# Two two-layer models on one core: mixer biases on GpSimd, a prepared final norm, reordered attention steps

## The chip, the core and the metric

The kernel runs on one core of a Trainium2 chip. The metric is device time in microseconds (us). TensorE (PE) does matmuls and transposes into PSUM (eight banks); VectorE (DVE) and ScalarE (ACT) do the rest; GpSimd (POOL) does small powers, some products and some transfers; the SP queue issues most transfers.

## The reference

Two models of two layers each, 256 positions, width 1024, fp32. `norm` is an RMS norm, `ffn` a gated feed-forward of width 2816.

```
for l in 0, 1:                                   # first model
    x = x + 0.5 * ffn(norm(x))
    p = norm(x) @ w_in + b_in                    # 5792 columns: three branches and 3 x 1024 gates
    y_a = lru_branch(p) @ lru_w_out
    y_b = latent_attention(p) @ mla_w_o          # 8 heads
    y_c = conv_branch(p) @ conv_w_out + conv_b_out
    x = x + (sig(g0) * y_a + sig(g1) * y_b + sig(g2) * y_c) @ w_out
    x = x + 0.5 * ffn(norm(x))
x = norm(x)                                      # second model
x = x + dilated_attention(norm(x)) @ a_w_out     # three dilations (1, 4, 16), each with its q, k, v; 16 heads,
                                                 # merged by their log-denominators
x = x + ffn(norm(x))
h = norm(x) @ b_w_in                             # q, k, v of 16 heads, and 16 columns of forget gates
c = cumsum(log_sigmoid(h[gates] + b_f))
x = x + attention(q, k, v, bias c_i - c_j) @ b_w_out
x = x + ffn(norm(x))
out = norm(x)
```

## The kernel before

All of x lies in SBUF as two tiles (t) of 128 positions. A matrix product is made in three passes: a weight slab of 128x1024 is loaded by SP (`raw`, five buffers), ACT rounds it to `H` (L378), DVE subtracts the rest `L` (L380), and PE multiplies H and L with the input's rounded part and H with its rest. `tm` has the input stationary and up to 512 weight columns moving, into two PSUM banks (one for each t) out of a ring; `fm` has the weights stationary. The stages follow one another: feed-forward, mixer, feed-forward, twice; the dilated attention; feed-forward; the forgetting attention ("fox"); feed-forward; the final norm.

In a **mixer** the order of the steps is the string `ORDER`. `gB`, `gA`, `gC` make the gates of the three branches (halves 0 and 1 of the columns), `yB`, `yA`, `yC` their output products (`combine`), summed in M. A gate is kept as tanh, so a branch adds (tanh + 1) times its product; M is halved later. `gate` loads its bias row of 1024 at half 0 into `bg`, which has one buffer; `combine_c` loads the convolution's bias into the same buffer and DVE adds it to the product (L917) ahead of the multiplication (L919) and the sum (L921). `pump` works off taps of the convolution on DVE (L861), `cn`, `cv`, `co` normalise it; `cv` ends in a power on POOL (`pow_rs`, L461). Two banks at a time come from a ring of three. Behind the last step M is transposed for `w_out`.

In **both attention stages** the steps of a group of heads are posted as jobs and run one by one between weight slabs (`tick`): `T` transposes q and k, `SC` makes scores, maximum and exponentials `P`, `U` transposes P and copies it to `PT`, `V` multiplies with v and normalises, `R` transposes the output and splits it. In dilations 4 and 16 (`banded`) four heads go together, in dilation 1 (`full`) and in fox (`pairs`) two. PE takes its instructions in the order written (`InOrder`); the other engines are ordered by the tile scheduler. In these stages `T`, `U` share a ring of two banks (3 and 6), `SC` has banks 4 and 5, `V` bank 7; `R` uses a strip of banks 4 and 5. In fox, `forget` makes the 16 gate columns with `tm` and their logarithms; `rows` makes the running sum and spreads it over the partitions through DRAM.

The **final norm** squares x (ACT, with a sum), takes a power on POOL for each t (`norm_scale`), and scales x times the gain.

Of the kernel before, what the change touches and what calls it, by code (L numbers as in the profile page):

```python
# [11 lines left out]
F32 = mybir.dt.float32  # L12
# [3 lines left out]
AF = mybir.ActivationFunctionType  # L16
# [3 lines left out]
S = 256  # L20
# [14 lines left out]
ORDER = ("rb glu:0 conv4:0 glu:1 latent conv4:1 lt gelu:0 pump:43 gelu:1 k:0 q:0 rk q:1 rq pump:6 lg:0 narrow "  # L35
         "gB:0 lg:1 k:1 pump:5 lg:2 lg:3 h:0 lru pump:14 gB:1 gA:0 h:1 h:2 h:3 gA:1 yB:0 yA:0 gC:0 yB:1 "
         "pump:52 cn cv yA:1 co gC:1 yC:0 yC:1")

# [205 lines left out]
class K:  # L244
# [217 lines left out]

    def norm_scale(self, t):
        nc, x = self.nc, self.x
        ss = self.sp.tile([128, 2], F32, name="ss1")
        ms = self.sp.tile([128, 1], F32, name="ms1")
        r = self.sp.tile([128, 1], F32, name="r1")
        for h in range(2):
            scr = self.sp.tile([128, 512], F32, name="scr", bufs=1)
            nc.scalar.activation(scr, x[:, t, 512 * h:512 * h + 512], AF.Square, accum_out=ss[:, h:h + 1])  # L470
        nc.vector.tensor_add(ms, ss[:, 0:1], ss[:, 1:2])
        nc.vector.tensor_scalar(ms, ms, 1.0 / D, EPS, op0=OP.mult, op1=OP.add)
        self.pow_rs(r, ms)
        return r

    def norm(self, gain):
# [218 lines left out]
    def mixer(self, l):  # L695
# [201 lines left out]
        def gate(b, i, n):  # L897
            j = (1, 0, 2)[i]
            if n == 0:
                bg[0] = p.tile([128, D], F32, name="bg", bufs=1)  # L900
                self.row(bg[0], A["b_in"], l * 5792 + 2720 + 1024 * j, D)
            g = gt[b]
            ns = slice(512 * n, 512 * n + 512)
            ps, = self.tm("w_in", l, [10 + 2 * i + n], XH, XL)
            for t in range(2):
                nc.vector.scalar_tensor_tensor(g[:, t, ns], ps[t], r[:, t:t + 1], bg[0][:, ns], op0=OP.mult, op1=OP.add)
            nc.scalar.activation(g[:, :, ns], g[:, :, ns], AF.Tanh, scale=0.5)

        def combine(name, b, YH, YL, n, bias=None):
            g = gt[b]  # L910
            ns = slice(512 * n, 512 * n + 512)
            ps, = self.tm(name, l, [n], YH, YL)
            for t in range(2):
                gs, src = g[:, t, ns], ps[t]
                if bias is not None:
                    y = ta.rearrange("p j s -> p (j s)")
                    nc.vector.tensor_add(y, ps[t], bias[:, ns])  # L917
                    src = y
                nc.vector.scalar_tensor_tensor(gs, gs, 1.0, src, op0=OP.add, op1=OP.mult)  # L919
                if b:  # L920
                    nc.vector.tensor_add(M[:, t, ns], M[:, t, ns], gs)  # L921

        def combine_c(n):
            if n == 0:
                bg[1] = p.tile([128, D], F32, name="bg", bufs=1)
                self.row(bg[1], A["conv_b_out"], l * D, D)
            combine("conv_w_out", 1, ycH, ycL, n, bias=bg[1])

# [7 lines left out]
            "yB": lambda n: combine("mla_w_o", 0, oH, oL, n), "yA": lambda n: combine("lru_w_out", 1, yaH, yaL, n),  # L936
            "yC": combine_c,
        }
# [25 lines left out]
    def final_norm(self, out):  # L964
        nc, x, g, xg = self.nc, self.x, self.gain, self.xg
        r = [self.norm_scale(t) for t in range(2)]
        for h in range(2):
            hs = slice(512 * h, 512 * h + 512)
            for t in range(2):
                nc.vector.tensor_mul(xg[:, t, hs], x[:, t, hs], g[:, hs])  # L970
        for t in range(2):
            for h in range(2):
                xs = xg[:, t, 512 * h:512 * h + 512]
                if h:
                    nc.vector.tensor_scalar(xs, xs, r[t], None, op0=OP.mult)
                else:
                    nc.scalar.activation(xs, xs, AF.Copy, scale=r[t])
                nc.sync.dma_start(out[0, 128 * t:128 * t + 128, 512 * h:512 * h + 512], xs)
        self.fin[0].close()
# [19 lines left out]
    def dilated(self):  # L999
# [59 lines left out]
        def banded(g, dil, hf, q, k):  # L1059
# [61 lines left out]

            early = [lambda: T(0), lambda: (T(1), SC(0)), lambda: (U(0), SC(1))]
            return early, lambda v: [lambda: (V(0, v), U(1)), lambda: (V(1, v), leave())]

        def full(hf, q, k):
# [27 lines left out]
            def U(i):  # L1153
                PT[i] = p.tile([128, 2, 2, 2, 128], F32, name="PT", bufs=2).rearrange("p a b c d -> p (a b c d)")[:, :768].rearrange("p (h c) -> p h c", h=2)
                for e in range(2):
                    tp = self.pt()[:, :384]
                    for b in range(3):
                        self.pe.transpose(tp[:, 128 * b:128 * b + 128], P[i][:, e, 128 * b:128 * b + 128], self.ident)
                    nc.vector.tensor_copy(PT[i][:, e], tp)  # L1159

# [31 lines left out]
            def R(i):  # L1192
                pb = self.bank[:, 4:6, 384:512]
                for t in range(2):
                    self.pe.transpose(pb[:, t], O[i][:, t], self.ident)
                h, lo = (z[:, 4 * hf + i].rearrange("p (t s) -> p t s", t=2) for z in (OH, OL))
                nc.scalar.copy(h, pb)
                nc.vector.tensor_sub(lo, pb, h.bitcast(F32))  # L1198

            early = [lambda: T(0), lambda: (T(1), SC(0)), lambda: (U(0), SC(1), T(2))]  # L1200
            return early, lambda v: [lambda: (V(0, v), U(1), SC(2), T(3)), lambda: (V(1, v), U(2), SC(3)),
                                     lambda: (V(2, v), R(0), U(3)), lambda: (V(3, v), R(1)), lambda: R(2), lambda: R(3)]

# [57 lines left out]
    def fox(self):  # L1261
# [10 lines left out]
        z = p.tile([128, 2, NH], F32, name="z")  # L1272

        def forget():
            e = p.tile([128, 2, NH], F32, name="e")
            ps, = self.tm("b_w_in_2", 0, [6], self.XH, self.XL)
            for t in range(2):
                nc.vector.scalar_tensor_tensor(z[:, t], ps[t], r[:, t:t + 1], bf, op0=OP.mult, op1=OP.add)
            nc.vector.scalar_tensor_tensor(e, z, -1.0, z, op0=OP.mult, op1=OP.max)
            nc.scalar.activation(e, e, AF.Exp, scale=-1.0)  # L1280
            l1p = self.log1p_exp(p, e.rearrange("p t h -> p (t h)"), 2 * NH, "lf")
            nc.vector.scalar_tensor_tensor(z, z, 0.0, l1p.rearrange("p (t h) -> p t h", t=2), op0=OP.min, op1=OP.subtract)
# [30 lines left out]
        def pairs(hf, q, k):  # L1313
# [12 lines left out]
            def SC(i):  # L1326
                P[i] = p.tile([128, 2, 384], F32, name="P", bufs=2)
                nm = p.tile([128, 2, 2], F32, name="nm", bufs=2)
# [18 lines left out]
            def U(i):  # L1347
                PT[i] = p.tile([128, 2, 384], F32, name="PT", bufs=2)
                for e in range(2):
                    tp = self.pt()[:, :384]  # L1350
                    for n in range(3):
                        self.pe.transpose(tp[:, 128 * n:128 * n + 128], P[i][:, e, 128 * n:128 * n + 128], self.ident)
                    nc.scalar.copy(PT[i][:, e], tp)

# [12 lines left out]
            def R(i):  # L1367
                pb = self.bank[:, 4:6, 384:512]
                for t in range(2):
                    self.pe.transpose(pb[:, t], O[i][:, t].rearrange("p h d -> p (h d)"), self.ident)  # L1370
                h, lo = (z[:, 4 * hf + i].rearrange("p (t s) -> p t s", t=2) for z in (OH, OL))
                nc.scalar.copy(h, pb)
                nc.vector.tensor_sub(lo, pb, h.bitcast(F32))

            early = [lambda: T(0), lambda: (SC(0), T(1)), lambda: (U(0), SC(1), T(2))]
            return early, lambda v: [lambda: (V(0, v), U(1), SC(2), T(3)), lambda: (V(1, v), U(2), SC(3)), lambda: (V(2, v), R(0), U(3)),
                                     lambda: (V(3, v), R(1)), lambda: R(2), lambda: R(3)]

        forget()
        self.post(5, rows)  # L1380
        for hf in range(2):
            late = []

            def each(i, a, q, k, v, hf=hf, late=late):
                if i == 1:
# [3 lines left out]
                    for n, job in enumerate(early):  # L1389
                        self.post((3 if hf else 5) + n, job)  # L1390
                if i == 2:
                    if hf == 0:
                        self.psum("pipe")
                    for job in late[0](v):
                        self.post(2, job)
            self.qkv(p, "b_w_in_2", 3 * hf, r, r8, HD, each=each)
# [66 lines left out]
```

## Time and profile before

| | us |
|---|---|
| median of three runs (2052.47 to 2054.57) | 2053.25 |
| profiled execution, its own time | 2052.71 |
| its span, first to last instruction | 2050.9 |
| PE busy | 2016.4 (98%) |
| DVE busy | 1314.3 (64%) |
| ACT busy | 1074.4 (52%) |
| POOL busy | 50.4 (2%) |

Busy time is that of instructions in work; matmuls are pipelined and their ends are modelled, so a stretch of full PE need not be PE at its highest rate. The mean granted clock of TensorE was 0.996 of full speed. A wait is the idle time of an engine ahead of an instruction, and the releaser is what ended it.

### The profile page before, as it was taken

Reading aid. Unit: us, or ns where it says so; the run is one execution under the profiler, and the core shown is the slowest. Engines: PE = TensorE matmul, PEld = TensorE weight load, DVE = VectorE, ACT = ScalarE, POOL = GpSimd, SP = SyncE. Lnnn points to the kernel's source line nnn. Section 1 sums busy time; section 2 is a strip of 40 time slices with the busy share of each in tenths; the row PEclk is TensorE's granted clock in tenths of the full one; section 3 lists DMA queues with packets and bytes.
Section 4 is the critical chain, followed back from the end, with each engine's and each line's share of the span. In section 5 each row is a group of like instructions: output and inputs, shape, how many; then the busy total and the mean of one; then the engine's idle time right before and its main releaser. Section 6 shows DMA issues by size and latency. Waiting matters only on the chain.

```text
span 2050.9 us, 27543 instructions
## 1 busy us (share of the span) xinstructions
PE 2016.4 (98%) x10496; PEld 1700.3 (83%) x10496; DVE 1314.3 (64%) x1994; ACT 1074.4 (52%) x1570; POOL 50.4 (2%) x70
## 2 busy tenths in 40 slices
PE   8999999999999999999999999999999999999998
PEld 7888988788888888988788887888778888788886
DVE  4565999865545556999755556666775555555554
ACT  5444685554445445675554456454554444555443
POOL 0000000000000000000000000000220000000000
PEclk9999999999999999999999999999999999999999
DMA  7566554556565556554556564555335564435653
GB/s 223 184 206 198 183 168 154 183 174 187 182 191 182 187 183 210 161 177 162 167 183 186 184 195 144 166 188 173 118 109 185 185 185 156 175 114 184 186 184 124
DMA packets 101700, 358.12 MB, mean 175 GB/s; under 512 B 13328, under 2 KB 14384, under 8 KB 101312
## 3 DMA queue, kind: packets, MB, share of 16 engines
q1 hardware_dynamic: 97312, 348.41, 53.9%
q0 software_dynamic: 4112, 7.72, 1.2%
q8 instruction: 82, 1.34, 0.3%
q10 hardware_dynamic: 144, 0.24, 0.1%
q14 instruction: 50, 0.41, 0.1%
HBM read 352.68 MB, written 3.23 MB: 174 GB/s over the span
## 4 chain that ended last, share of the span: by engine, by line
PE 84%; DVE 7%; issue 5%; ACT 3%; DMA 1%; POOL 0%; POOLq 0%; ACTq 0%; DVEq 0%
PE bank L215 80%; PE bank L218 4%; DVE L L380 2%; ACT H L378 1%; DVE acc L861 1%; DMA bg<-in_conv_b_out 0%; DVE xa L803 0%; DMA pi<-in_positions 0%; DMA h<-in_masks 0%; ACT XN L1031 0%; ACT P L1150 0%; DVE fr L457 0%; ACT cs L889 0%; DVE ta L917 0%; ACT XH L456 0%
## 5 line engine op out<-in xcount | busy, mean ns | idle before, releaser
L380 DVE TENSOR_TENSOR L<-raw,H 128x1024 fp32r<-128x1024 f32 (+1 forms) x653 | 794.0, 1217 | 644.3 <-ACT H L378 642.4
L378 ACT CAST H<-raw 128x1024 fp32r<-128x1024 f32 (+1 forms) x653 | 682.5, 1046 | 829.0 <-PE bank L215 796.2
L215 PE MATMUL bank<-H,XH 128*128 128x512 f32 (+3 forms) x1680 | 636.0, 379 | 2.7 <-ACT H L378 2.6
L215 PE MATMUL bank<-L,XH 128*128 128x512 f32 (+3 forms) x1680 | 630.1, 375 | 1.1 <-DVE L L380 1.1
L215 PE MATMUL bank<-H,XL 128*128 128x512 f32 (+3 forms) x1680 | 627.0, 376 | 0.0
L215 PEld LDWEIGHTS bank<-H,XH 128*128 128x128 f32 x1680 | 316.9, 189 | 58.6 <-ACT H L378 2.8
L215 PEld LDWEIGHTS bank<-L,XH 128*128 128x128 f32 x1680 | 317.2, 189 | 55.7 <-DVE L L380 2.7
L215 PEld LDWEIGHTS bank<-H,XL 128*128 128x128 f32 x1680 | 315.7, 189 | 55.8 <-DVE XL L457 1.4
L215 PE MATMUL bank<-H,HH 128*128 128x512 f32 x528 | 206.5, 391 | 0.0
L215 PE MATMUL bank<-H,HL 128*128 128x512 f32 x528 | 205.5, 389 | 0.0
L215 PE MATMUL bank<-L,HH 128*128 128x512 f32 x528 | 205.4, 389 | 0.0
L215 PEld LDWEIGHTS bank<-H,HL 128*128 128x128 f32 x528 | 99.1, 188 | 20.8
L215 PEld LDWEIGHTS bank<-H,HH 128*128 128x128 f32 x528 | 99.5, 188 | 20.1
L215 PEld LDWEIGHTS bank<-L,HH 128*128 128x128 f32 x528 | 99.2, 188 | 20.2
L861 DVE SCALAR_TENSOR_TENSOR acc<-cpad,cvec,acc 128x256 f32<-128x256 f32 x240 | 104.2, 478 | 0.0
L215 PE MATMUL bank<-H,XP 128*128 128x512 f32 x256 | 85.0, 403 | 0.2 <-DVE XP L1198 0.2
L215 PE MATMUL bank<-XH,H 128*128 128x256 f32 x256 | 70.9, 282 | 0.1
L215 PE MATMUL bank<-XH,L 128*128 128x256 f32 x256 | 71.0, 280 | 0.0
L215 PE MATMUL bank<-XL,H 128*128 128x256 f32 x256 | 70.1, 281 | 0.0
L215 PE MATMUL bank<-H,XN 128*128 128x512 f32 x192 | 63.1, 398 | 0.0
L215 PEld LDWEIGHTS bank<-H,XP 128*128 128x128 f32 x256 | 48.7, 191 | 11.2 <-DVE XP L1198 0.8
L215 PEld LDWEIGHTS bank<-v,PT 128*128 128x128 f32 x416 | 51.7, 191 | 3.7 <-DVE PT L1159 0.7
(333 smaller groups left out, 2027.9 us busy)
## 6 DMA issues: line engine op xcount, KB each, us to landing
raw<-in_ffn_w SPq DMA_DIRECT2D x264, 512.0 KB, 3.5
raw<-in_ffn_w_gu SPq DMA_DIRECT2D x88, 512.0 KB, 3.6
raw<-in_w_in SPq DMA_DIRECT2D x80, 512.0 KB, 3.5
raw<-in_a_w_in SPq DMA_DIRECT2D x72, 512.0 KB, 3.7
raw<-in_ffn_w_down SPq DMA_DIRECT2D x44, 512.0 KB, 3.6
raw<-in_b_w_in SPq DMA_DIRECT2D x24, 512.0 KB, 3.5
raw<-in_w_out SPq DMA_DIRECT2D x16, 512.0 KB, 3.5
raw<-in_mla_w_o SPq DMA_DIRECT2D x8, 512.0 KB, 3.5
```

The lines of the kernel that those rows point to most:

```text
L215: self._next(self.tc.nc.tensor.matmul(*args, **kw))
L218: self._next(self.tc.nc.tensor.transpose(*args, **kw))
L378: nc.scalar.copy(H[:, :nw], raw[:, :nw])
L380: nc.vector.tensor_sub(L[:, :nw], raw[:, :nw], H[:, :nw].bitcast(F32))
L861: nc.vector.scalar_tensor_tensor(acc[:, c], cpad[:, c, tap:tap + S], dww[:, tap, c:c + 1], acc[:, c], op0=OP.mult, op1=OP.add)
```

## The change

In the mixers a gate's bias comes as two halves of 512, and `bg` has two buffers. Two new steps stand in `ORDER`: `bM` loads half of the convolution's bias and adds it to M on POOL; `bC` multiplies it on POOL with the gate and adds that to M. DVE's addition of the bias (L917) goes. In the final norm the first halves are squared for both tiles first and their part of the mean is kept in `pre`. In `banded`, `full` and `pairs` the parts of the jobs are in another order, half of the PT copies change engine, and R of odd heads uses the ring of T and U. In fox `forget` has the weights stationary and the arithmetic on its result is a job of its own (`gates`); U comes one job later, with a third buffer for P; the jobs of the second half of the heads are posted earlier.

```diff
-         ... gA:1 yB:0 yA:0 gC:0 yB:1 pump:52 cn cv yA:1 co gC:1 yC:0 yC:1
+         ... gA:1 yB:0 yA:0 gC:0 bM:0 bC:0 yB:1 pump:52 cn cv yA:1 bM:1 co gC:1 yC:0 bC:1 yC:1
...
         def gate(b, i, n):
-            if n == 0:
-                bg[0] = p.tile([128, D], F32, name="bg", bufs=1)
-                self.row(bg[0], A["b_in"], l * 5792 + 2720 + 1024 * j, D)
+            bias = p.tile([128, 512], F32, name="bg", bufs=2)
+            self.row(bias, A["b_in"], l * 5792 + 2720 + 1024 * j + 512 * n, 512)
...
+        def bias(n):
+            ns = slice(512 * n, 512 * n + 512)
+            bg[n] = p.tile([128, 512], F32, name="bg", bufs=2)
+            self.row(bg[n], A["conv_b_out"], l * D + 512 * n, 512)
+            for t in range(2):
+                nc.gpsimd.tensor_add(M[:, t, ns], M[:, t, ns], bg[n])
+        def gate_bias(n):
+            ns = slice(512 * n, 512 * n + 512)
+            tb = ta.rearrange("p j s -> p (j s)")
+            for t in range(2):
+                m = M[:, t, ns]
+                nc.gpsimd.tensor_mul(tb, gt[1][:, t, ns], bg[n])
+                nc.gpsimd.tensor_add(m, m, tb)
...
-                gs, src = g[:, t, ns], ps[t]
-                if bias is not None:
-                    y = ta.rearrange("p j s -> p (j s)")
-                    nc.vector.tensor_add(y, ps[t], bias[:, ns])
-                    src = y
-                nc.vector.scalar_tensor_tensor(gs, gs, 1.0, src, op0=OP.add, op1=OP.mult)
+                gs = g[:, t, ns]
+                nc.vector.scalar_tensor_tensor(gs, gs, 1.0, ps[t], op0=OP.add, op1=OP.mult)
...
     def final_norm(self, out):
-        r = [self.norm_scale(t) for t in range(2)]
         for h in range(2):
+            for t in range(2):
+                nc.scalar.activation(scr, x[:, t, hs], AF.Square, accum_out=ss[:, t, h:h + 1])
+                if h:
+                    nc.vector.scalar_tensor_tensor(ms[:, t:t + 1], ss[:, t, 1:2], 1.0 / D, pre[:, t:t + 1], op0=OP.mult, op1=OP.add)
+                    self.pow_rs(r[t], ms[:, t:t + 1])
+                else:
+                    nc.vector.tensor_scalar(pre[:, t:t + 1], ss[:, t, 0:1], 1.0 / D, EPS, op0=OP.mult, op1=OP.add)
...
         def banded(g, dil, hf, q, k):
-            early = [lambda: T(0), lambda: (T(1), SC(0)), lambda: (U(0), SC(1))]
+            early = [lambda: T(0), lambda: (T(1), SC(0)), lambda: (SC(1), U(0))]
...
         def full(hf, q, k):                      # U; R is changed alike in pairs
-                    nc.vector.tensor_copy(PT[i][:, e], tp)
+                    (nc.vector.tensor_copy if e else nc.scalar.copy)(PT[i][:, e], tp)
-                pb = self.bank[:, 4:6, 384:512]
+                pb = self.pt()[:, :S].rearrange("p (t s) -> p t s", t=2) if i % 2 else self.bank[:, 4:6, 384:512]
-            early = [lambda: T(0), lambda: (T(1), SC(0)), lambda: (U(0), SC(1), T(2))]
-            return early, lambda v: [lambda: (V(0, v), U(1), SC(2), T(3)), lambda: (V(1, v), U(2), SC(3)),
+            early = [lambda: T(0), lambda: (T(1), SC(0)), lambda: (T(2), SC(1), U(0))]
+            return early, lambda v: [lambda: (T(3), SC(2), V(0, v), U(1)), lambda: (SC(3), V(1, v), U(2)),
                                      lambda: (V(2, v), R(0), U(3)), lambda: (V(3, v), R(1)), lambda: R(2), lambda: R(3)]
...
         def forget():
-            ps, = self.tm("b_w_in_2", 0, [6], self.XH, self.XL)
+            ps = self.pt()[:NH, :S]
+            H, L = self.slab("b_w_in_2", 0, 6, 0, 8)
+            for k in range(8):
+                self.pe.matmul(ps, H[:, k, :], self.XH[:, k, :], start=k == 0, stop=False)
+                self.pe.matmul(ps, L[:, k, :], self.XH[:, k, :], start=False, stop=False)
+                self.pe.matmul(ps, H[:, k, :], self.XL[:, k, :], start=False, stop=k == 7)
+            nc.vector.tensor_copy(zt, ps)
+        def gates():
+            for t in range(2):
+                self.pe.transpose(ps[:, t], zt[:, 128 * t:128 * t + 128], self.ident[:NH, :NH])
...
         def pairs(hf, q, k):
-                P[i] = p.tile([128, 2, 384], F32, name="P", bufs=2)
+                P[i] = p.tile([128, 2, 384], F32, name="P", bufs=3)
-                    nc.scalar.copy(PT[i][:, e], tp)
+                    (nc.vector.tensor_copy if e else nc.scalar.copy)(PT[i][:, e], tp)
-            early = [lambda: T(0), lambda: (SC(0), T(1)), lambda: (U(0), SC(1), T(2))]
-            return early, lambda v: [lambda: (V(0, v), U(1), SC(2), T(3)), lambda: (V(1, v), U(2), SC(3)), lambda: (V(2, v), R(0), U(3)),
-                                     lambda: (V(3, v), R(1)), lambda: R(2), lambda: R(3)]
+            early = [lambda: T(0), lambda: (T(1), SC(0)), lambda: (T(2), SC(1))]
+            return early, lambda v: [lambda: (T(3), SC(2), U(0)), lambda: (V(0, v), SC(3), U(1)), lambda: (V(1, v), U(2)),
+                                     lambda: (V(2, v), R(0), U(3)), lambda: (V(3, v), R(1)), lambda: (R(2), R(3))]
         forget()
+        self.post(2, gates)
         self.post(5, rows)
-                        self.post((3 if hf else 5) + n, job)
+                        self.post((2 if hf else 5) + n, job)
-                        self.post(2, job)
+                        self.post(2 - hf, job)
```

## Rows read from the trace of the kernel before

**Rows 1.** Stretches: us; PE, PEld, DVE, ACT, POOL busy (instructions); clock; DMA share; GB/s.

```profile
206.00:412.00 206.00, 203.38 (x1204) 178.41 (x1205) 189.83 (x350) 131.27 (x219) 3.37 (x4) 1.00 0.54 169
430.00:617.00 187.00, 187.00 (x901) 156.95 (x900) 100.71 (x103) 88.87 (x107) 0.69 (x1) 1.00 0.60 186
...
1221.00:1532.00 311.00, 300.83 (x1654) 246.45 (x1653) 211.11 (x421) 166.76 (x276) 30.32 (x38) 0.99 0.48 151
...
1720.00:1857.00 137.00, 131.63 (x762) 109.09 (x760) 78.37 (x160) 78.06 (x161) 2.39 (x4) 0.98 0.43 143
```

**Rows 2.** Waits of PE, whole span: us in total, times, longest.

```profile
PE bank L218 <- DVE PT L1159: 4.8, 2, 2.4
PE bank L218 <- ACT P L1345: 2.9, 3, 1.6
...
PE bank L218 <- DVE gt L921: 2.1, 2, 1.0
PE bank L218 <- ACT v L991: 1.7, 1, 1.7
PE bank L218 <- DVE XP L1198: 1.6, 2, 1.3
...
PE bank L218 <- ACT P L1089: 1.3, 1, 1.3
...
PE bank L215 <- DVE ta L917: 1.1, 2, 0.7
```

**Rows 3.** Two stretches of the first mixer, DVE alone; columns as in rows 1.

```profile
344.00:364.00 20.00, 19.79 (x33) 1.00 0.64 203
364.00:404.00 40.00, 30.30 (x39) 1.00 0.59 183
```

**Rows 4.** Timeline, end of the first mixer: start, us, engine, line, operation [idle before].

```profile
393.43 0.33 SPq L295 DMA_DIRECT2D bg<-in_conv_b_out  x1
...
398.52 0.69 DVE L917 TENSOR_TENSOR ta<-bank,bg 128x512 f32<-128x512 f32 x1 [1.72 <-DMA bg<-in_conv_b_out]
...
399.27 0.50 PE L215 MATMUL bank<-H,ycH 128*128 128x512 f32 x1 [0.73 <-DVE ta L917]
...
399.86 1.22 DVE L380 TENSOR_TENSOR L<-raw,H 128x1024 fp32r<-128x1024 f32 x1
```

**Rows 5.** Timeline of POOL in the dilated stage.

```profile
1441.65 1.18 POOL L1187 TENSOR_TENSOR O<-Y,w 128x256 f32<-128x256 f32 x2 [24.80 <-DVE w L1183]
...
1445.14 2.17 POOL L1187 TENSOR_TENSOR O<-Y,w 128x256 f32<-128x256 f32 x2 [1.49 <-DVE w L1183]
```

**Rows 6.** Timeline of DVE at the same time.

```profile
1445.31 1.52 DVE L380 TENSOR_TENSOR L<-raw,H 128x1024 fp32r<-128x1024 f32 x1
```

**Rows 7.** Timeline of PE in the dilated stage, second half of the heads.

```profile
1501.07 0.44 PE L218 MATMUL bank<-ident,q 128*128 128x128 f32 x2 [2.45 <-DVE PT L1159]
```

**Rows 8.** Stretches of PE alone, dilated stage and start of fox; clock is third.

```profile
1502.00:1505.00 3.00, 3.00 (x8) 0.50 0.26 104
1727.00:1734.00 7.00, 7.00 (x23) 0.52 0.14 35
```

**Rows 9.** Timeline of PE in fox, matmuls of `forget`, first and last of 29.

```profile
1723.64 0.26 PE L215 MATMUL bank<-H,XH 128*128 128x16 f32 x1
...
1726.77 0.26 PE L215 MATMUL bank<-L,XH 128*128 128x16 f32 x1
```

**Rows 10.** A stretch of the first mixer in which PE runs 256-column matmuls.

```profile
207.00:230.00 23.00, 23.00 (x199) 1.00 0.58 178
```

**Rows 11.** Timeline of the final norm.

```profile
2042.95 0.69 DVE L568 SCALAR_TENSOR_TENSOR x<-bank,x 128x512 f32<-128x512 f32 x1
...
2044.37 0.19 ACT L470 ACTIVATION_READ_ACCUMULATOR scr<-x 128x1 f32 x1
...
2045.50 0.15 DVE L472 TENSOR_SCALAR ms<-ms 128x1 f32<-128x1 f32 x1
...
2045.73 0.55 POOL L461 TENSOR_TENSOR r<-ms,half 128x1 f32<-128x1 f32 x1 [0.66 <-DVE ms L472]
```

More of the change, by code (lines that the diff above doesn't have):

```diff
@@ L35 @@
 ORDER = ("rb glu:0 conv4:0 glu:1 latent conv4:1 lt gelu:0 pump:43 gelu:1 k:0 q:0 rk q:1 rq pump:6 lg:0 narrow "
-         "gB:0 lg:1 k:1 pump:5 lg:2 lg:3 h:0 lru pump:14 gB:1 gA:0 h:1 h:2 h:3 gA:1 yB:0 yA:0 gC:0 yB:1 "
-         "pump:52 cn cv yA:1 co gC:1 yC:0 yC:1")
+         "gB:0 lg:1 k:1 pump:5 lg:2 lg:3 h:0 lru pump:14 gB:1 gA:0 h:1 h:2 h:3 gA:1 yB:0 yA:0 gC:0 bM:0 bC:0 yB:1 "
+         "pump:52 cn cv yA:1 bM:1 co gC:1 yC:0 bC:1 yC:1")
 def _span(a, b, w):
@@ L461, in pow_rs @@
         self.nc.gpsimd.tensor_tensor(out, ms, self.half[:, 0:1].to_broadcast([128, n]), op=OP.pow)
[L463 to L474, printed above, removed]
     def norm(self, gain):
@@ L905, in gate, with combine @@
             for t in range(2):
-                nc.vector.scalar_tensor_tensor(g[:, t, ns], ps[t], r[:, t:t + 1], bg[0][:, ns], op0=OP.mult, op1=OP.add)
+                nc.vector.scalar_tensor_tensor(g[:, t, ns], ps[t], r[:, t:t + 1], bias, op0=OP.mult, op1=OP.add)
             nc.scalar.activation(g[:, :, ns], g[:, :, ns], AF.Tanh, scale=0.5)
-        def combine(name, b, YH, YL, n, bias=None):
+        def bias(n):
[11 more added lines that the diff above has]
+                nc.gpsimd.tensor_add(m, m, tb)
+        def combine(name, b, YH, YL, n):
             g = gt[b]
@@ L913, in combine @@
             for t in range(2):
-                gs, src = g[:, t, ns], ps[t]
-                if bias is not None:
-                    y = ta.rearrange("p j s -> p (j s)")
-                    nc.vector.tensor_add(y, ps[t], bias[:, ns])
-                    src = y
-                nc.vector.scalar_tensor_tensor(gs, gs, 1.0, src, op0=OP.add, op1=OP.mult)
+                gs = g[:, t, ns]
+                nc.vector.scalar_tensor_tensor(gs, gs, 1.0, ps[t], op0=OP.add, op1=OP.mult)
                 if b:
                     nc.vector.tensor_add(M[:, t, ns], M[:, t, ns], gs)
[L923 to L927, printed above, removed]
         steps = {
@@ L936, in mixer @@
             "yB": lambda n: combine("mla_w_o", 0, oH, oL, n), "yA": lambda n: combine("lru_w_out", 1, yaH, yaL, n),
-            "yC": combine_c,
+            "yC": lambda n: combine("conv_w_out", 1, ycH, ycL, n), "bM": bias, "bC": gate_bias,
         }
@@ L965, in final_norm @@
         nc, x, g, xg = self.nc, self.x, self.gain, self.xg
-        r = [self.norm_scale(t) for t in range(2)]
+        ss = self.sp.tile([128, 2, 2], F32, name="ss")
+        pre = self.sp.tile([128, 2], F32, name="pre", bufs=1)
+        ms = self.sp.tile([128, 2], F32, name="ms")
+        r = [self.sp.tile([128, 1], F32, name=f"rf{t}", bufs=1) for t in range(2)]
         for h in range(2):
             hs = slice(512 * h, 512 * h + 512)
+            for t in range(2):
+                scr = self.sp.tile([128, 512], F32, name="scr", bufs=1)
+                nc.scalar.activation(scr, x[:, t, hs], AF.Square, accum_out=ss[:, t, h:h + 1])
[4 more added lines that the diff above has]
+                    nc.vector.tensor_scalar(pre[:, t:t + 1], ss[:, t, 0:1], 1.0 / D, EPS, op0=OP.mult, op1=OP.add)
             for t in range(2):
@@ L1272, in fox @@
         z = p.tile([128, 2, NH], F32, name="z")
+        zt = p.tile([NH, S], F32, name="zt")
         def forget():
+            ps = self.pt()[:NH, :S]
[6 more added lines that the diff above has]
+        def gates():
             e = p.tile([128, 2, NH], F32, name="e")
-            ps, = self.tm("b_w_in_2", 0, [6], self.XH, self.XL)
+            ps = self.pt()[:, :2 * NH].rearrange("p (t h) -> p t h", t=2)
             for t in range(2):
-                nc.vector.scalar_tensor_tensor(z[:, t], ps[t], r[:, t:t + 1], bf, op0=OP.mult, op1=OP.add)
+                self.pe.transpose(ps[:, t], zt[:, 128 * t:128 * t + 128], self.ident[:NH, :NH])
+            for t in range(2):
+                nc.vector.scalar_tensor_tensor(z[:, t], ps[:, t], r[:, t:t + 1], bf, op0=OP.mult, op1=OP.add)
             nc.vector.scalar_tensor_tensor(e, z, -1.0, z, op0=OP.mult, op1=OP.max)
@@ L1367, in R @@
             def R(i):
-                pb = self.bank[:, 4:6, 384:512]
+                pb = self.pt()[:, :S].rearrange("p (t s) -> p t s", t=2) if i % 2 else self.bank[:, 4:6, 384:512]
                 for t in range(2):
```

## The prediction

> **What bounds the kernel now.** I read the profiled execution by stages first. In a feed-forward stage TensorE (PE) is busy for all of its 187.00 us; in the first mixer it is idle for 206.00 - 203.38 = 2.6 us, in the dilated stage for 10.2, in the forgetting stage ("fox") for 5.4 [rows 1]. So the span is PE's time nearly everywhere, the six feed-forward stages hold nothing to gain, and this change touches none of them. What it can give is PE's idle time in the four other stages, matmuls that are saved, stretches at a low clock, and the tail behind the last matmul.
>
> Then the list of what PE waited for, whole span [rows 2]. It names the places that the diff touches: the copies of transposed probabilities (PT, L1159) 4.8 us in two waits, exponentials (P) in fox 2.9 and in the banded part 1.3, M's last additions (L921) 2.1, the evacuation of v 1.7, the second half of the output split (L1198) 1.6, the sum with the convolution's bias (L917) 1.1. Last, VectorE (DVE) in a mixer: 19.79 of 20.00 us busy while the taps are pumped, 30.30 of 40.00 after [rows 3]. Inside a mixer DVE is a second bound just under PE.
>
> **Mixers: bias and gated part to GpSimd.** The convolution's bias now waits in the SP queue for a buffer and goes out at 393.43; L917 idles 1.72 us for it and takes 0.69, and the next matmul, which needs the PSUM bank that L917 reads, waits 0.73 [rows 4]. The change drops L917: four per mixer, 4 x 0.69 = 2.8 us off DVE, off the chain from the last matmul to M as well. The bias is fetched in halves into two buffers, long before its use. So the waits on L917 and on L921, 1.1 + 2.1 = 3.2 us in both mixers [rows 2], can go: **-3.2**.
>
> What it adds: 12 GpSimd operations of 128x512 per mixer, all with two SBUF inputs (4 for the bias, 8 for its product with the gate). The trace has none so wide. The nearest rows are those of 128x256 in the dilated stage: two take 1.18 us alone, so I estimate 1.2 for one of 512; beside DVE two took 2.17 [rows 5]. DVE paid too: a split of a weight slab (L380), also with two SBUF inputs, took 1.52 beside them [rows 6] against 1.22 [rows 4]. That is 0.30 us lost to DVE per slab, 0.6 if it doubles with the width. From below the cost is nothing, since GpSimd is otherwise idle in a mixer and DVE idles for 9.7 of the 40 us in which ten of the twelve fall [rows 3]; from above it is all 1.2 us of each on PE's path. I take the row's 0.6 for the two of `bM:1`, which run while `co` prepares the operand of `yC:0` that PE needs next, and nothing for the others, which have slabs split ahead to eat: 1.2 us a mixer, **+2.4**. GpSimd's queue also holds `cv`'s power, which `co` waits for; it stands behind `bC:0`, whose gate `gC:0` is two steps of TensorE work ahead of it, and ahead of `bM:1`; held back, it would hold back `co` by as much. On SP each mixer issues eight half rows for four whole ones, 4 x 0.33 us more issue [rows 4] on a queue that only issues; what stands behind a row that waits for its buffer are slab loads, five deep. I cost that at nothing; a late slab would cost PE what it is late.
>
> On the shared port the row shows contention of some tenths [rows 5, 6]. The Trainium skill, page "SBUF — State Buffer", section "SBUF: two separate sides", is harsher: DVE with two SBUF inputs and GpSimd lock the port pair for the whole instruction, and the loser blocks. By that rule each of the 24 could hold DVE for its whole length. The stretched slab agrees in kind, not in size. What such a lock would make of the time is a rival below.
>
> **Dilated stage.** In `full` the transposes of q and k (T(3)) stand behind U(1), whose two PT copies wait in DVE's queue; PE idles 2.45 us there [rows 7], in both halves: 4.8 [rows 2]. Now T, then the scores, come first and V and U last; T's bank was emptied a step before, and half of the copies go to ScalarE: **-4.8**. Right after one of the two waits the granted clock is 0.50 for 3.00 us, the 1.2 GHz level, with PE's idle time ahead of it [rows 8]; without that wait I expect the 2.4 GHz level, half of some 3.3 us: **-1.6**. R(odd) gets a bank of its own ring, so R no longer waits for L1198: **-1.6**. In `banded` the scores go ahead of U(0), which hides the wait for exponentials: **-1.3**. What is late next: V(2) now starts one slab after U(2), and the scores of a step need the banks that the exponentials of the step before read. Bounds: nothing, or the same 7.7 us of waits again. I hand back **+1.5**, nearer nothing, as a slab of matmuls lies between each pair. Net -7.8.
>
> **Fox.** `forget` issues 48 matmuls of 16 moving columns. They start every 0.112 us: 29 of them from 1723.64 to 1726.77 [rows 9]. The new form turns the operands round: 24 of 256 columns. Fp32 matmuls with 256 columns run at 23.00 us / 199 = 0.116 us [rows 10]. So 48 x 0.112 = 5.4 becomes 24 x 0.116 = 2.8, plus 0.2 for two transposes: **-2.4**. Behind the run of 16-column matmuls the clock is 0.52 for 7 us [rows 8]; 7.00 x 0.48 = 3.4 us are lost, 0.2 of it on matmuls already counted. Dense matmuls there should keep the upper level: **-3.2**. `forget` no longer takes two banks of the main ring, so T(0) finds another bank than v's: **-1.7**. U goes one step later, behind the next scores: the wait for P, **-2.9** [rows 2]. The gate arithmetic moves two steps back; it is small DVE work which only `rows` needs. In the second half of the heads all steps are posted one slab earlier, so that T(0) has one slab of matmuls less to cover k's evacuation; I cost that at nothing, and at a wait of v's size, 1.7, if the cover fails. Handed back, as V now starts one slab after U: **+1.5**, between nothing and 4.6. Net -8.7.
>
> **Final norm.** The last half of x is there at 2042.95 + 0.69 = 2043.64; its square's sum is read by 2044.56, as the square of the tile's first half, known long before, stands ahead of it on ScalarE; then two DVE operations, the second at 2045.50 behind a scaling, and the power, to 2046.28 [rows 11]. After: the first halves are squared early, so the sum comes 0.2 sooner, at 2044.4; one DVE operation of 0.15, a power of 0.55 and hops of 0.1 give 2045.2. **-1.1**.
>
> **Sum.** -0.8 - 7.8 - 8.7 - 1.1 = -18.4. The profiled execution takes 2052.71 us by its own time, 1.8 around a span of 2050.9; 2052.71 - 18.4 = 2034.3. The median of the runs, 2053.25, lies 0.5 higher: **2035 us**.
>
> **Rivals.**
> *The waits move in place of going.* Half of the attention waits (4.8 + 1.6 + 1.3 + 1.7 + 2.9, 12.3 in all) come back at V or at the scores, 6.2 where I hand back 3.0, and both low stretches of the clock stay, 1.6 + 3.2 = 4.8: 2035 + 3.2 + 4.8 = 2043. For it: DVE feeds every one of these steps. Against it: DVE idles in fox and PT is shared now. Chance 0.16.
> *Contention eats the mixers.* Every GpSimd operation costs PE 0.6: 24 x 0.6 - 3.2 = +11.2 for -0.8: 2047. For it: DVE at 19.79 of 20 [rows 3]. Against: only the first two additions fall there. Chance 0.13.
> *Hardly any change:* both of these together leave under 4 us. Chance 0.07.
> *Slower: GpSimd locks DVE.* Place: `bM` and `bC` in both mixers. Each operation stops DVE for its full 1.2 us and PE with it: 24 x 1.2 = 28.8, less the 3.2 of waits, +25.6 for -0.8, so 2061. It decides from (17.6 + 3.2) / 24 = 0.87 us per operation on; below that the other stages outweigh it. Only DVE's idle quarter and the slabs split ahead stand against it. Chance 0.06. It is what the rule of the SBUF page would give if DVE never had slack.
>
> **How the numbers follow.** The forecast has the other 0.58. Its own range is 2029 (nothing handed back: 9.3 + 10.2 + 3.2 + 1.1 = 23.8) to 2040. The range, 2026 to 2047, takes in the first two rivals and 3 us below for short waits that the list does not name; it leaves out little more than the last two. Faster by over 0.2% (4 us, about what a measurement of this kernel can tell from no change): 0.58 + 0.16 + 0.13 = 0.87; within it 0.07; slower 0.06.
>
> **What would show it.** In the profile after: no PE wait on PT copies, on P in fox, on v or on a bias; PE's idle time under 5 us in the dilated stage and under 3 in fox; a clock of 1.00 through fox's start; that stage some 9 us shorter. In the mixers GpSimd busy for 14 us or more each, slabs beside it stretched, and PE's waits on L921 gone. Wrong it would be made by PE waits on PT or on scores of the old size at V, by a mixer longer than 206 us, or by a low clock at fox's start.

## The result, and the profile after

Before: 2052.86 us (median of 4 runs beside those of after). After: 2087.78 us (2087.01 to 2088.67, 4 runs). The ratio is 1.0169, 95% interval 1.0156 to 1.0182: the change makes the kernel slower by 34.9 us, where 18 us of gain were predicted.

First the stages. The norm's power on GpSimd ends each of them, so the distance from one power to the next is a stage's length. Worked out from the starts of those rows (us):

| | mixer 1 | feed-forward | mixer 2 | dilated | feed-forward | fox | last feed-forward |
|---|---|---|---|---|---|---|---|
| before | 229.4 | 187.2 | 229.0 | 302.8 | 187.1 | 137.2 | 183.1 |
| after | 238.7 | 188.9 | 236.9 | 320.2 | 188.8 | 130.0 | 184.0 |

Fox gains 7.1 us. The mixers lose 9.3 and 7.8, the dilated stage 17.4, and the feed-forward stages, in which no instruction is changed, some 1.7 each (the last one shows less, because the change also starts the first power of the final norm 0.7 earlier).

Stretches of after, columns as in [rows 1]: a mixer, a feed-forward stage, the dilated stage, fox.

```profile
206.00:412.00 206.00, 201.40 (x1171) 175.99 (x1170) 190.62 (x338) 129.12 (x216) 26.09 (x16) 0.98 0.52 164
440.50:627.50 187.00, 187.00 (x887) 155.33 (x886) 99.28 (x103) 87.09 (x104) 0.70 (x1) 1.00 0.59 184
1245.00:1572.00 327.00, 310.97 (x1647) 252.69 (x1648) 203.93 (x411) 169.39 (x280) 32.04 (x38) 0.97 0.46 142
1762.00:1892.00 130.00, 126.53 (x740) 104.28 (x739) 81.48 (x169) 74.52 (x154) 2.38 (x4) 1.00 0.47 151
```

In the feed-forward stage PE is busy for all of the 187.00 us, as before, and has 887 matmuls in them for 901 [rows 1]: it does not wait, each matmul takes longer. In the mixer and the dilated stage the clock is 0.98 and 0.97, no longer 1.00 and 0.99. In fox it is now 1.00, as predicted. The waits of PE in after, against [rows 2]:

```profile
PE bank L215 <- DVE PT L1105: 11.1, 8, 3.0
PE bank L215 <- ACT cs L860: 3.8, 2, 1.9
PE bank L215 <- DVE gt L892: 2.8, 4, 0.8
...
PE bank L218 <- DVE gt L918: 2.4, 2, 1.2
...
PE bank L218 <- ACT qk L1342: 2.0, 2, 1.3
PE bank L215 <- DVE XP L1202: 2.0, 2, 1.4
PE bank L218 <- DVE gt L920: 1.6, 4, 0.5
...
PE bank L215 <- DVE OL L1391: 1.3, 1, 1.3
```

The waits on `full`'s PT (4.8 us), P in fox (2.9), v (1.7) and the bias (1.1) are gone. New are `banded`'s PT (L1105, 11.1), the squares of the convolution (L860, 3.8) and the gates' bank (L892, 2.8); M's last additions (L918, L920) are 4.0 instead of 2.1.

**In the mixer.** GpSimd and then DVE of after, in the same microseconds of the first mixer:

```profile
370.03 1.30 POOL L909 TENSOR_TENSOR ta<-gt,bg 128x512 f32<-128x512 f32 x1 [8.96 <-ACT gt L893]
371.40 2.14 POOL L910 TENSOR_TENSOR gt<-gt,ta 128x512 f32<-128x512 f32 x1
373.62 1.28 POOL L909 TENSOR_TENSOR ta<-gt,bg 128x512 f32<-128x512 f32 x1
374.98 2.15 POOL L910 TENSOR_TENSOR gt<-gt,ta 128x512 f32<-128x512 f32 x1
```

```profile
371.08 1.33 DVE L380 TENSOR_TENSOR L<-raw,H 128x1024 fp32r<-128x1024 f32 x1 [1.09 <-ACT H L378]
372.33 1.27 DVE L918 SCALAR_TENSOR_TENSOR gt<-gt,bank 128x512 f32<-128x512 f32 x2
373.87 2.11 DVE L380 TENSOR_TENSOR L<-raw,H 128x1024 fp32r<-128x1024 f32 x1 [0.27 <-ACT H L378]
375.90 2.31 DVE L859 TENSOR_TENSOR acc<-acc,rb 128x1024 f32<-128x1024 f32 x1
```

The subtraction that ends them, in the kernel before:

```profile
373.41 1.22 DVE L872 TENSOR_TENSOR acc<-acc,rb 128x1024 f32<-128x1024 f32 x1
```

Where the two engines overlap, the instruction that begins second is stretched. A GpSimd operation takes 1.28 to 1.30 us when it begins undisturbed, 2.14 or 2.15 when it begins beside a DVE operation with two SBUF inputs; such a DVE operation takes 2.11 or 2.31 instead of 1.22 when it begins beside one of GpSimd. L918, which reads one operand from PSUM, takes 1.27 for two beside them, and its forerunner takes 1.28 for two before, without them. The subtraction L859 ends at 378.21, before at 374.63, in mixers that begin within 0.1 us of each other; the squares, the variance's matmuls and PE stand behind it (PE, then its clock, third, of a stretch right behind):

```profile
379.35 3.12 PE L215 MATMUL bank<-ones,cs 128*128 128x1 f32 x16 [1.88 <-ACT cs L860]
```

```profile
380.00:386.00 6.00, 6.00 (x21) 0.50 0.32 107
```

PE stands still for 1.9 us and then runs 6.8 us at the 1.2 GHz level, another 3.4 lost. At the mixer's end it happens again: DVE's addition L920 takes 1.78 instead of 0.68, M is late, and 3.4 us at the low level follow the wait.

**In the dilated stage.** DVE of after in a `banded` group, then PE's V (L1105 is the copy of PT, L1091, L1092 and L1096 the softmax of SC(1) and of the group's first half, L380 a slab):

```profile
1296.13 0.68 DVE L1105 COPY PT<-bank 128x512 f32<-128x512 f32 x1
1296.73 0.68 DVE L1092 TENSOR_TENSOR P<-bank,X 128x512 f32<-128x512 f32 x1
1297.51 1.23 DVE L380 TENSOR_TENSOR L<-raw,H 128x1024 fp32r<-128x1024 f32 x1
1298.65 1.27 DVE L1096 TENSOR_REDUCE X<-P 128x4 f32<-128x512 f32 x2
1299.84 0.68 DVE L1105 COPY PT<-bank 128x512 f32<-128x512 f32 x1
```

```profile
1300.57 2.02 PE L215 MATMUL bank<-v,PT 128*128 128x64 f32 x12 [3.05 <-DVE PT L1105]
```

U(0) is issued behind SC(1), so its second copy stands in DVE's queue behind a slab and SC(1)'s own operations; V(0) needs it one slab (12 matmuls, 2.7 us) later and waits 3.05 us, and 2.3 in each of the other three group halves.

**In the feed-forward stages.** Matmul groups of after whose moving operand is XH (first) or the hidden activations HH, HL: busy us, mean ns.

```profile
L215 PE MATMUL bank<-L,XH 128*128 128x512 f32 (+2 forms) x1664 | 625.8, 376 | 1.1 <-DVE L L380 1.1
...
L215 PE MATMUL bank<-L,HH 128*128 128x512 f32 x528 | 210.7, 399 | 0.0
L215 PE MATMUL bank<-H,HH 128*128 128x512 f32 x528 | 209.0, 396 | 0.0
L215 PE MATMUL bank<-H,HL 128*128 128x512 f32 x528 | 207.0, 392 | 0.0
```

Before, the same three groups have means of 389, 391 and 389 ns. From one start to the next the trace has a median (the pitch) of 227 ns for all of them before; after, 237, 232 and 231, and still 227 for XH. XH lies in a pool that the change does not move. HH and HL lie in a stage's own pool, which is laid out behind the pool of small tiles: the change takes six places of 32 bytes out of that one (ss1, ms1, r1, twice each) and puts three in (pre, rf0, rf1), so every stage's buffers start 96 bytes lower, 160 past a multiple of 256 instead of on one.

### The profile page after: what moved, and what is told of

It reads as the page before. It is cut to its first block, busy times and chain, and to the rows that moved or that the text cites. A ratio compares the mean times of both kernels' runs of the same rounds, so it can differ in the third digit from the quotient of the medians.

```text
span 2086.9 us, 27550 instructions
## 1 busy us (share of the span) xinstructions
PE 2041.9 (98%) x10474; PEld 1708.3 (82%) x10474; DVE 1324.2 (63%) x1987; ACT 1073.8 (51%) x1570; POOL 97.9 (5%) x94
## 4 chain that ended last, share of the span: by engine, by line
PE 83%; DVE 8%; issue 5%; ACT 4%; POOL 0%; DMA 0%; POOLq 0%; ACTq 0%; DVEq 0%
PE bank L215 78%; PE bank L218 4%; DVE L L380 3%; ACT H L378 2%; DVE acc L848 1%; DVE gt L920 1%; DVE xa L790 0%; ACT XH L456 0%; DMA h<-in_masks 0%; DVE acc L859 0%; DVE PT L1105 0%; ACT XN L1035 0%; ACT cs L876 0%; ACT P L1154 0%; DVE fr L457 0%
## 5 line engine op out<-in xcount | busy, mean ns | idle before, releaser
L380 DVE TENSOR_TENSOR L<-raw,H 128x1024 fp32r<-128x1024 f32 (+1 forms) x653 | 800.7, 1227 | 663.2 <-ACT H L378 661.9
L215 PE MATMUL bank<-H,XH 128*128 128x512 f32 (+2 forms) x1664 | 633.0, 380 | 2.3 <-ACT H L378 2.2
L215 PE MATMUL bank<-L,XH 128*128 128x512 f32 (+2 forms) x1664 | 625.8, 376 | 1.1 <-DVE L L380 1.1
L215 PE MATMUL bank<-H,XL 128*128 128x512 f32 (+2 forms) x1664 | 622.7, 376 | 0.2
L215 PE MATMUL bank<-L,HH 128*128 128x512 f32 x528 | 210.7, 399 | 0.0
L215 PE MATMUL bank<-XH,H 128*128 128x256 f32 (+1 forms) x264 | 73.1, 282 | 0.1
L215 PE MATMUL bank<-XH,L 128*128 128x256 f32 (+1 forms) x264 | 73.1, 279 | 0.0
L215 PE MATMUL bank<-XL,H 128*128 128x256 f32 (+1 forms) x264 | 72.4, 281 | 0.2
L215 PE MATMUL bank<-v,PT 128*128 128x64 f32 x416 | 56.1, 285 | 11.1 <-DVE PT L1105 11.1
```

What stands on the lines that cost most here:

```text
L215: self._next(self.tc.nc.tensor.matmul(*args, **kw))
L380: nc.vector.tensor_sub(L[:, :nw], raw[:, :nw], H[:, :nw].bitcast(F32))
```

## The experiments

| run | us | before beside it | ratio, 95% interval |
|---|---|---|---|
| aligned | 2072.81 | 2052.03 | 1.0097 (1.0082 to 1.0112) |
| shifted | 2065.68 | 2052.03 | 1.0067 (1.0052 to 1.0082) |
| mixers | 2067.46 | 2052.03 | 1.0072 (1.0057 to 1.0087) |
| banded | 2072.68 | 2052.03 | 1.0097 (1.0080 to 1.0114) |
| full | 2048.60 | 2053.32 | 0.9972 (0.9960 to 0.9984) |
| fox | 2047.14 | 2053.32 | 0.9965 (0.9953 to 0.9977) |
| final | 2054.73 | 2053.32 | 1.0003 (0.9994 to 1.0012) |
| kept | 2040.10 | 2053.32 | 0.9934 (0.9922 to 0.9947) |
| dead | 2070.59 | 2053.32 | 1.0083 (1.0065 to 1.0102) |
| mixers_dve | 2053.92 | 2053.32 | 1.0003 (0.9994 to 1.0012) |
| banded_act | 2053.87 | 2053.32 | 1.0004 (0.9994 to 1.0013) |

The runs that were timed once (kept_rows, off32, off64, off128) stand with their text; kept_rows is the kernel of `kept` again.

**The place of the buffers.** `aligned`, on the changed kernel, and `shifted`, on the kernel before (there with 40 for 24):

```diff
     def final_norm(self, out):
         nc, x, g, xg = self.nc, self.x, self.gain, self.xg
+        self.sp.tile([128, 24], F32, name="pad", bufs=1)
```

> The changed kernel with one unused tile of 96 bytes added to the pool of small tiles, so that every stage's buffers start again where they start in the kernel before (on a multiple of 256 bytes instead of 160 past one). Theory A (place of the buffers): the matmuls that read HH and HL go from 231 to 237 ns start to start back to 227, each feed-forward stage from 188.8 to 187.1 us, XN, XP and fr likewise; about 528 x 19 ns = 10.0 us for HH and HL and some 5 for the others, so 2072 to 2074 us. Theory B (the feed-forward stages are slower through something that the mixers leave behind, the queues or the transfers): no change, 2088 us.

> The kernel before with nothing changed but one unused tile of 160 bytes in the pool of small tiles, which puts every stage's buffers at the same offset within 256 bytes as the changed kernel has them. Theory A: 2053 + 10 + 5 = 2066 to 2069 us, with HH and HL matmuls at 231 to 237 ns. Theory B: 2053 us.

Taking the displacement away gives 2087.78 - 2072.81 = 15.0 us back; adding it alone costs 13.7 (0.3 less than the least that was expected). The group of matmuls with L and HH, first of `aligned`, then of `shifted`:

```profile
L215 PE MATMUL bank<-L,HH 128*128 128x512 f32 x528 | 205.4, 389 | 0.0
```

```profile
L215 PE MATMUL bank<-L,HH 128*128 128x512 f32 x528 | 209.4, 397 | 0.0
```

The feed-forward stages are 187.2 us in `aligned` and 188.9 in `shifted`. Theory A holds, B falls. Three more kernels ask which offset costs it; each is the kernel before with another size of the unused tile (8, 16 and 32 in place of 40: 32, 64 and 128 bytes).

> The kernel before with an unused tile of 32 bytes, which puts every stage's buffers 32 bytes past a multiple of 256. If multiples of 64 bytes are what counts, HH and HL matmuls at 231 to 237 ns start to start and 2065 to 2068 us, as with 160 bytes (which is 32 past a multiple of 64); if the distance to 256 counts, some other pitch above 227.

> The same with 64 bytes. If multiples of 64 bytes count, 227 ns and 2051 to 2055 us, as before; if multiples of 128 or 256 count, 231 ns or more and above 2060 us.

> The same with 128 bytes. If multiples of 64 or of 128 bytes count, 227 ns and 2051 to 2055 us; if multiples of 256 count, above 2060 us.

2065.75, 2065.04 and 2066.29 us, beside one run of before of 2054.71; the median pitch of HH and HL is 232 to 235, 235 to 236 and 232 ns. All three are 10 to 12 us slower than the run of before beside them, so of the starts that were tried only a multiple of 256 bytes gives 227.

**One part at a time.** `mixers`, `full`, `fox` and `final` are the kernel before with the lines of that part in the diff (`final` with the tile of 24 as well); `banded` is this line, the only one that the change alters there (its copies of PT all stay on DVE):

```diff
-            early = [lambda: T(0), lambda: (T(1), SC(0)), lambda: (U(0), SC(1))]
+            early = [lambda: T(0), lambda: (T(1), SC(0)), lambda: (SC(1), U(0))]
```

> The kernel before with the mixers' part of the change alone (bias and gated bias on GpSimd, rows in two buffers), the buffers where they were. The prediction gave this part -0.8 us: 2052. Theory now: the GpSimd operations hold the DVE operations beside them for their whole 1.28 us, pump ends late, PE waits 2.3 us at the convolution's variance and 2.3 at the transposes of M, and each wait is followed by a stretch at half clock: +7 to +8 us a mixer, 2067 to 2069. Rival: the mixers are slower through the place of their buffers, then 2053.

> The kernel before with one line changed: in the banded groups U(0) is issued behind SC(1) instead of ahead of it. The prediction gave this -1.3 us: 2051.5. Theory now: the copy of PT stands on DVE behind the softmax of SC(1), so the first V of each of the four group halves waits 2.5 to 3.3 us, and a stretch of 3.4 to 6.8 us at half clock follows each: 10.9 + up to 10.2 - 1.3 = +15 to +20, so 2068 to 2073 us. Rival: the waits come from the other parts (ring of banks in the full group), then 2051 to 2053.

> The kernel before with the full group's part alone (T(2), SC(1), U(0) reordered, T(3) ahead of V(0), PT copied by both engines, R in a ring bank for odd heads). The prediction gave -4.8 - 1.6 - 1.6 + 1.5 = -6.5: 2045.5 us. Theory now: the same, since the waits for PT of 2.4 us at T(3) are gone in the trace after; 2044 to 2047 us. Rival: the bank that R takes out of the ring is missed by the others, within 2 us of before, 2050 to 2054.

> The kernel before with the second model's attention part alone (forget gates with wide moving operand, three P buffers, reordered jobs). The prediction gave -8.7: 2043.4 us. From the stage's span in the trace after, 131 against 137 us with its buffers displaced: -6 to -8, so 2044 to 2046 us. Rival: what the gates save is used up by the transposes of zt and the later posts: 2050 to 2053.

> The kernel before with the final norm's part alone, and an unused tile of 96 bytes so that all other buffers stay where they were. The prediction gave -1.1: 2051. Theory: 2050.5 to 2052, hardly to be told from before. Rival: the multiplications by the gain now stand beside the power on GpSimd, whose first one took 0.99 instead of 0.55 us after: +0.5, 2052.5 to 2053.

By stage, from the same rows as the table at the top: `mixers` makes the mixers 236.7 and 236.6 us long, +7.3 and +7.6; `banded` the dilated stage 322.8, +20.0; `full` makes that 297.2, -5.6; `fox` makes its stage 129.6, -7.6; `final` shortens the last stage and the tail by 0.3. The sum, 14.9 + 20.0 - 5.6 - 7.6 - 0.3 = 21.4, is near what `aligned` lost against before, 20.8; with 15.0 for the place it is 36.4, against 34.9 measured. The whole times of the last three say -4.7, -6.2 and +1.4, each with the stage's value inside its interval; `full` and `fox` lie 1 to 2 us above what was expected of them, and `final` cannot be told from before. Executions differ by low stretches of the clock that come and go where nothing was changed: `full` has one of 3.4 us in its first mixer. In `banded` the waits of PE are these, and the clock (third column) is low behind all four, by one row of each:

```profile
PE bank L215 <- DVE PT L1101: 11.2, 8, 3.1
```

```profile
1280.00:1283.00 3.00, 3.00 (x13) 0.59 0.00 0
1320.00:1327.00 7.00, 6.49 (x26) 0.51 0.24 75
1372.00:1375.00 3.00, 3.00 (x11) 0.56 0.01 5
1419.00:1422.00 3.00, 3.00 (x14) 0.50 0.27 107
```

The trace has 3.4, 6.8, 3.4 and 3.4 us at the low level there; half of 17.0 is 8.5; with the waits of 11.2, less the 1.3 for P that are gone, that is 18.4 of the 20.0. The rest is about what one more low stretch of 3.4 us costs, behind an old wait on `full`'s PT: before has a low stretch behind one of these two waits [rows 8], `banded` behind both. So have `mixers` and `final`, and their dilated stage, in which nothing is changed, takes 304.2 us for 302.8. The waits of PE that are new in `mixers`:

```profile
PE bank L215 <- ACT cs L873: 4.1, 2, 2.0
PE bank L215 <- DVE gt L905: 3.2, 4, 0.9
...
PE bank L218 <- DVE gt L931: 2.4, 2, 1.2
...
PE bank L218 <- DVE gt L933: 2.0, 4, 0.5
```

They are 11.7 us; less the 3.2 on L917 and L921 [rows 2], which are gone, 8.5. Four stretches of 3.4 us at the low level, two a mixer, lose another 6.8: 15.3 for the 14.9 that the stages show.

**What the GpSimd operations cost.** `dead` leaves before's mixers as they are and adds the 12 operations a mixer, with results that nobody reads; `mixers_dve` is `mixers` with `nc.vector` for `nc.gpsimd` in `bias` and `gate_bias`.

```diff
+        a, b = (z.rearrange("p a b c -> p (a b c)") for z in (q, kf))
+        def dead_M(n):
+            for t in range(2):
+                nc.gpsimd.tensor_add(a[:, :512], M[:, t, 512 * n:512 * n + 512], b[:, :512])
+        def dead_C(n):
+            for t in range(2):
+                nc.gpsimd.tensor_mul(a[:, 512:1024], gt[1][:, t, 512 * n:512 * n + 512], b[:, :512])
+                nc.gpsimd.tensor_add(a[:, :512], a[:, :512], a[:, 512:1024])
```

> The kernel before, its mixers as they were, and in each of them the changed kernel's 12 GpSimd operations at the same places, on the same inputs M and gt, with results that go to a buffer which nobody reads any more. Theory A (a GpSimd operation holds the DVE operation beside it): nothing waits for the results, and still DVE loses about 1 us to each; since DVE also keeps the four additions that the change takes away, the loss is that of the mixers' part or more: 2066 to 2073 us. Theory B (the mixers' part costs time because M and the gate are now handed between two engines): 2052 to 2055 us.

> The mixers' part alone, as in the run of that name, with its 12 operations a mixer issued on DVE in place of GpSimd. They take some 0.68 us each there: 12 x 0.68 - 4 x 0.69 = 5.4 us more work a mixer for an engine that is at 97 to 99% there. Theory A: cheaper than the same operations on GpSimd, which cost DVE 1.0 to 1.1 us each; six of them ahead of the variance are 4.1 us in place of 6.3, so that the wait of 2.0 us there is about gone; +1 to +4 a mixer, 2055 to 2061 us. Theory B (work moved off DVE helps, whatever it holds): slower than on GpSimd, above 2067.

`dead` costs 17.3 us, 7.6 and 7.7 in the two mixers by its trace, with no result of GpSimd read by another engine: theory A, not B. PE waits there for the squares (4.1 us in two) as in `mixers`, and for the old L921:

```profile
PE bank L218 <- DVE gt L921: 4.9, 2, 2.6
```

`mixers_dve` can't be told from before; its mixers take 229.8 us each, +0.4 and +0.7. That is less than theory A asked for: the 12 operations take 0.68 or 0.69 us each on DVE, L872 ends at 375.55 us (378.21 in after, whose mixer begins 0.4 later), and no wait for the squares is left. So the same arithmetic costs next to nothing on the engine that was to be relieved, and 14.9 us beside it.

**The banded copy.** `banded` with one copy of two on ScalarE:

```diff
-                    nc.vector.tensor_copy(PT[i][:, e], tp)
+                    (nc.scalar.copy if e else nc.vector.tensor_copy)(PT[i][:, e], tp)
```

> The run called banded (U(0) behind SC(1)), with the second of the two copies of PT on ACT. Theory: V waits because that copy stands in DVE's queue behind a weight subtraction and four operations of SC(1)'s softmax; on ACT it stands behind two exponentials and ends some 1.5 to 2 us earlier, so that the waits of 2.5 to 3.1 us fall to 0.5 to 1.5 and the clock hardly falls: 2058 to 2065 us. Rival: V waits for the transposes themselves, which come late on PE, then 2071 to 2074 as before.

```profile
PE bank L215 <- DVE PT L1101: 1.4, 4, 0.5
```

The waits fall from 11.2 to 1.4 us, no low clock is left in the groups, and the time is that of before: better than expected, as the earlier 1.3 us of waiting for P (L1089) is gone too. The place of the copy in DVE's queue made the wait; the transposes did not.

**What is worth keeping.** `kept` is the changed kernel with the tile of 24 and with the mixers and `banded` as before.

> The changed kernel with the mixers and the banded groups' order as they were before and the unused tile of 96 bytes: what is left of the change is the full group, the second model's attention and the final norm. If the parts add up: -6.5 - 7 - 1 = -14.5, so 2036 to 2039 us, faster than both kernels. Rival: the parts are not additive, since each stage starts on what the one before it leaves in its queues: 2040 to 2046.

> The kernel called kept once more, one look only, to see how its stages stand in a second profile: 2038 to 2042 us.

2040.10 us, 13.2 less than before, and 2038.41 when run again: faster than both kernels. It lies 1 us above the range, as I had taken the final norm for 1 us; -5.6 - 7.6 - 0.3 = -13.5 is what the stages say.

## Why the prediction was wrong

The mixers and `banded` were mis-sized with the wrong sign, one effect was not in the sum at all, and the parts that were right in kind in the attention stages came out 13 to 14% smaller.

- **"the six feed-forward stages hold nothing to gain, and this change touches none of them".** It touches none of their instructions, but it moves their buffers: 15.0 us, about 10 of it in these six stages (1.7 each); for the rest, an estimate: the 816 matmuls that move XN, XP and fr have a median pitch of 231 to 234 ns in after for 227 before, together some 4 us. The diff showed the cause, three small tiles that go; I costed only what the instructions do. The kernel itself gave a hint: its class `Pool` rounds each tile of type fp32r to `LINE = 256` bytes, and a tile of 192 bytes that nothing reads, `lead2`, stands in the pool of small tiles; the change left both as they were.
- **Mixers, "nothing for the others, which have slabs split ahead to eat".** Predicted -0.8, measured +14.9. The estimate of 1.2 us for the operation was near (1.28 to 1.30); the 0.6 us that DVE loses was too little, 0.9 to 1.1 measured where the two overlap (2.11, 2.31 against 1.22; 1.78 against 0.68). And I looked for cover in the wrong place: slabs ahead cover PE's weights, not the chain from the taps over L859 and the squares to the variance, which DVE feeds and during whose taps it has 0.2 us of slack in 20 [rows 3]; six operations delay it. PE then waits and loses clock on top. (The 206 us in the list of signs is a stretch that was read; the mixer takes 229.4 before.) What the Trainium skill says of it, "SBUF — State Buffer", section "SBUF: two separate sides" (the shared port pair is held for a whole instruction, against a DVE operation with two SBUF inputs), agrees with 2.11 to 2.31 for 1.22, and with L918, which has one input in PSUM and is not stretched. I weighed that rule against a row of 128x256 [rows 5, 6], whose operations of half the width stretched the slab by 0.30.
- **`banded`, "the scores go ahead of U(0), which hides the wait for exponentials: -1.3"**, with "a slab of matmuls lies between each pair". Predicted -1.3, measured +20.0. The 1.3 did go, but what became late next was the copy, on an engine's queue that I did not write out: a slab of matmuls covers 12 x 0.227 = 2.7 us, and from the end of U's transposes (1293.6 in after) to the end of the second copy (1300.5) it is 6.9. The prediction named PE waits on PT at V as what would prove it wrong; it is what came.
- **`full`: -6.5 predicted, -5.6 measured.** The waits on PT (4.8) and the low clock behind one of them went, as said. **"R(odd) gets a bank of its own ring, so R no longer waits for L1198: -1.6"** failed: R doesn't wait, but the output projection now waits 2.0 us for the same split of XP, which is its operand.
- **Fox: -8.7 predicted, -7.6 measured.** 24 matmuls start every 0.113 us, as the row said; the clock is 1.00, the waits on v and P are gone. Handed back are 2.0 us behind qk's evacuation (L1342) and a wait on OL of 1.3 (0.6 before), for which 1.5 was allowed.
- **Final norm: -1.1 predicted, 0.3 measured.** The one operation that is left of the mean (L969) is issued behind the scaling of the other tile, just as its forerunner was [rows 11]: the sum is read at 2080.62, L969 starts at 2081.37. And the first power takes 0.98 us beside a DVE multiplication, 0.55 alone.
- **The rivals.** The one on the other side, GpSimd locking DVE, was right in kind and carried 0.06. Of its 28.8 us 18.1 came (the 14.9, and the 3.2 of waits that went as predicted), 6.8 of them as low clock; PE loses only where a result of DVE comes late for it. By itself it would have used up the gain and little more (14.9 - 5.6 - 7.6 - 0.3 = +1.4); `banded` and the place of the buffers made the rest. The rival of waits that move to V was right in kind for `banded` and too small (6.2 us of waits come back, 11.2 measured there); the place of the buffers stands in none.

## What to carry to other kernels

Before work is moved to GpSimd, ask what DVE does at that moment and whether its operands are in SBUF: an idle engine is not free if its operations stretch those of the busy one (here 1.22 us to 2.31). When a step is moved behind another, write out the queue of the engine that ends it, not only that of TensorE, and follow it to the first instruction that reads the result; the 11.2 us of waits in `banded` cost another 8.5 in clock. And read a diff for what it does to the layout: tiles that come or go in one pool displace all pools behind it, which shows in stages that the diff does not touch.

## What the runs showed of the hardware

A matmul's pitch goes with the start of its moving operand. 128x512 matmuls start every 227 ns when the operand's buffer begins on a multiple of 256 bytes; every 231 to 237 ns when it begins 32, 64, 128 or 160 bytes past one (`off32`, `off64`, `off128`, `shifted`), with the same instructions and a granted clock of 1.00. All buffers of a stage were moved together; that it is the moving operand is read from the matmuls with XH in the same stages, whose buffer was not moved and whose pitch stays at 227 with weights in the same buffers (H and L). No run shows why.

A short stop of PE can be followed by a second loss: behind each of the waits of 2.3 to 3.1 us in `banded` the granted clock was at its lower level, 1.2 GHz, for 3.4 or 6.8 us, though PE was busy behind it. It need not be: of the two waits of 2.4 us on `full`'s PT before, only one has a low stretch behind it [rows 8].
